# The last phase of a streaming encoder layer: y's scale from a bound, y split and transposed in halves, gates loaded later, two transposes on other PSUM banks

## The chip, the cores and the metric

One core of a Trainium2 chip. The metric is the device time of one execution in microseconds (us). The engines are named as in the profile: PE (TensorE) multiplies, PEld loads its weights, DVE is VectorE, ACT is ScalarE, POOL is GpSimd, SP issues the DMAs.

## The reference

One layer of a chunk-causal encoder for 2048 prompt frames and 8 x 16 sample frames with caches of 512. Each frame is normalised and modulated, projected by `w_in`, and goes through two attention branches (differential and stick-breaking). The last phase of the kernel computes the merge and the output of each frame:

```python
def merge_branches(oa, ob, za, zb, ga, gb, subln_g, lam_init, w_branch_a, w_branch_b, w_out):
    b, s = oa.shape[:2]
    oa = rms_norm(oa, subln_g) * (1.0 - lam_init)
    ya = (oa.reshape(b, s, WIDTH_A) * jax.nn.silu(za)) @ w_branch_a
    yb = (ob.reshape(b, s, WIDTH_B) * jax.nn.silu(zb)) @ w_branch_b
    return (jax.nn.sigmoid(ga) * ya + jax.nn.sigmoid(gb) * yb) @ w_out
...
        xp = xp + gate * merge_branches(oa, ob, za, zb, ga, gb, subln_g[l], lam_init,
                                        w_branch_a[l], w_branch_b[l], w_out[l])
...
    y_prompt = rms_norm(xp, final_g)
```

Below, u is the gated attention output (what the branch weights multiply, 1024 wide), y is the merged sum (what `w_out` multiplies, 1024 wide), and g are the two gates `ga`, `gb`.

## The kernel before

All large products run on PE in 16-bit halves: an operand is scaled by a power of two per row, rounded to 16 bits (the high part), and the rest is rounded too (the low part); a product is three matmuls, high x high, high x low and low x high. `split` makes the two parts: one instruction on the engine given (here ACT) for the high part, one on DVE for the low part. The power of two comes from `scales`, a handful of operations on one column, from the sum of squares of the row, so that nothing overflows.

The kernel goes through eight units of projection and attention, and then, from about 1790 us of the profile on, through the last phase, which is what the diff touches; the tail of the last unit already runs its first tiles (`early_work`). The rows are cut into 17 tiles of 128 frames, in the order `tiles`: 15 prompt tiles, the sample tile, the last prompt tile. Iteration n of the last loop has these pieces of work, written in this order (the document uses the short names):

- b(n), `branches`: four groups of 12 matmuls of 512 columns (L1202), for each column half j both branches br. Each group is scaled and gated on DVE into the gate's own buffer (L1204); after the second branch the two are added on POOL (L1206), which gives a half of y. When both halves are there, `finish` takes their sums of squares on ACT (L274), makes y's scale `sy`, and splits both halves (L287 on ACT, L292 on DVE) into one buffer `y16`.
- T(n+1), `turned`: one DMA transpose of u of the next tile (L1191), 16 blocks of 128 x 128.
- inputs(n+2): loads o_d, z_d (L1158, L1159) and the gates g_d in two halves (L1163); sigmoid of z on ACT into banks of tag mm, products on POOL (L1170) and DVE (L1172, L1176), sigmoid of g on ACT (both L120), sum of squares, scale and split of u. The buffers `hs[0]`, `hs[1]` (o, z) and `hs[2]` (split u) are single.
- o(n-1), `output`: two groups of 24 matmuls of 512 columns (L1335) for the tile before, then the scaling on DVE (L1339), the residual on POOL (L1343), the last norm and the store.
- Ty(n), `turned_y`: one DMA transpose of y's two parts (L1227), 16 blocks, into the single buffer `L["y"]`.

Beside that, `aside(n)` deals out the work of the sample's attention in small steps (`sample`): `keys` turns cached keys on PE (L735), in turn into a PSUM bank of tag t and one of tag s, and copies them out (L736, DVE and ACT); `queries` turns the sample's queries (L721); `weights` turns the attention weights, four blocks in a bank s (L770) and the last block in a bank t (L776). The PSUM has two banks of tag mm, three of tag s, one of tag t and two of tag o. The sample's work lasts for the first 13 of the iterations.

What runs when: `interleave` merges the lists by their shares of cost into one written order. A planner (`schedule_with_timeline_sim=True`) then orders the instructions of each engine and of each queue by its own simulated times, and every engine runs its list strictly in that order. So an instruction that waits holds up all that stand behind it on its engine, and SP's DMAs stand in one such list. The activations that need a table (sigmoid, exp) are tied to each other in their written order (`act`).

Of the kernel before, what the change touches and what calls it, by code (L numbers as in the profile page):

```python
# [25 lines left out]
P = 128  # L26
D = 1024
# [83 lines left out]
def layer_kernel(ctx: ExitStack, tc: tile.TileContext, a: dict):  # L111
# [589 lines left out]
    def sample(U, dec, fixed):  # L701
# [14 lines left out]
            load(out=kc, in_=caches[name][:, i * 8 : i * 8 + 8, h * P : (h + 1) * P])  # L716

        def queries():
            pt = bank("t")
            for j in range(2):  # L720
                T.transpose(pt[:, j * P : (j + 1) * P], box["s"][:, j * P : (j + 1) * P], ident)  # L721
# [44 lines left out]
        def weights(c):  # L766
            w = box["jobs"][c]["segs"][0]["p"]
            pt = bank("s")
            for j in range(4):
                T.transpose(pt[:, j * P : (j + 1) * P], w[:, j * P : (j + 1) * P], ident)  # L770
# [5 lines left out]
            T.transpose(pt[:, 0:P], w[:, 512:640], ident)  # L776
            S.copy(out=wn[:, c, :], in_=pt[:, 0:P])

# [376 lines left out]
    def inputs(t):  # L1155

        o, z = hs[0:2]
        load(out=o, in_=o_d[t])  # L1158
        load(out=z, in_=z_d[t])  # L1159
        gs = []  # L1160
        for j in range(2):
            gs.append(L["g"][(2 * len(begun) + j) % 4].rearrange("p (b n) -> p b n", b=2))
            load(out=gs[j], in_=g_d[t].rearrange("p (b n) -> p b n", b=2)[:, :, j * 512 : (j + 1) * 512])  # L1163
        begun.append(t)
        r = L["orms"][:, 4 * t : 4 * t + 4] if t < NT else rsqrt(osums[:, NT, :], 4, P, tiny, "rA")
        for n in range(2):
            c = slice(n * 512, (n + 1) * 512)
            sg = bank("mm")
            act(out=sg, in_=z[:, c], func=AF.Sigmoid)
            G.tensor_tensor(out=o[:, c], in0=o[:, c], in1=z[:, c], op=ALU.mult)  # L1170
            if n == 1:
                V.tensor_tensor(out=o[:, c], in0=o[:, c], in1=sg, op=ALU.mult)  # L1172
            else:
                for h in range(4):
                    c = slice(h * P, (h + 1) * P)
                    V.scalar_tensor_tensor(out=o[:, c], in0=sg[:, c], scalar=r[:, h : h + 1], in1=o[:, c], op0=ALU.mult, op1=ALU.mult)  # L1176
# [9 lines left out]
        return dict(u16=u16, u=L["u"][len(begun) % 2], iu=iu, g=gs)  # L1186

    def turned(st):

# [3 lines left out]
    def branches(st):  # L1193

        def half(j, br):
# [8 lines left out]
            V.scalar_tensor_tensor(out=g, in0=pb, scalar=st["iu"], in1=g, op0=ALU.mult, op1=ALU.mult)  # L1204
            if br == 1:
                G.tensor_tensor(out=g, in0=st["g"][j][:, 0, :], in1=g, op=ALU.add)  # L1206
                if j == 1:
                    finish()

        def finish():  # L1210
            acc = tiny.tile([P, 2], F32, tag="yacc", name="yacc")
            for j in range(2):
                sum_squares(st["g"][j][:, 1, :], 512, acc[:, j : j + 1])
            sy = scales(add_up(acc, 2), unit, "sy")
            y16 = L["y16"].bitcast(F16).rearrange("p (f n) -> p f n", f=2)
            for j in range(2):
                c = slice(j * 512, (j + 1) * 512)
                split(y16[:, 0, c], y16[:, 1, c], st["g"][j][:, 1, :], sy[:, 0:1], S)
            iy = unit.tile([P, 1], F32, tag="iy", name="iy")
            V.tensor_tensor(out=iy, in0=sy[:, 1:2], in1=L["s"][1][:, 1:2], op=ALU.mult)  # L1220
            st["y16"], st["iy"] = y16, iy

        return [(2.6, lambda j=j, br=br: half(j, br)) for j in range(2) for br in range(2)]

    def turned_y(st):
        st["y"] = yT = L["y"].bitcast(F16).rearrange("p (k n) -> p k n", n=P)
        nc.sync.dma_start_transpose(out=yT, in_=st["y16"].rearrange("p f n -> p (f n)"))  # L1227


    tiles = list(range(NT - 1)) + [NT, NT - 1]  # L1230
# [2 lines left out]
    def branch_weight():  # L1233

        i = branch_weights.pop(0)
        if i == 0:
            L["s"] = [scales(total(add_up(wsums[:, lo : lo + 8], 8)), con, f"s_w{lo}") for lo in (0, 8)]
# [8 lines left out]
    def early_work():  # L1246


        free.extend(units[7]["bufs"])

        def first(t):
            if "orms" not in L:
                L["orms"] = rsqrt(osums[:, 0:NT, :].rearrange("p t h -> p (t h)"), 4 * NT, P, con, "orms")
            states[t] = inputs(t)
            if t == tiles[0]:
                turned(states[t])

        def early(i):

            if i == 0:  # L1260
                L["first"] = [fn for _, fn in branches(states[tiles[0]])] + [lambda: turned_y(states[tiles[0]])]
            L["first"][i]()

        def rest():
            L["g"], L["u"], (L["y"], L["y16"]) = free[0:4], free[4:6], free[6:8]

        return [branch_weight for _ in branch_weights] + [rest] + [lambda t=t: first(t) for t in tiles[0:2]] \
            + [lambda i=i: early(i) for i in range(5)]

    for n in range(first_step, len(steps) + PV_LAG):  # L1270
        if n < len(steps):
# [24 lines left out]
    with ExitStack() as c2:  # L1296
# [25 lines left out]
        def output(t, st):  # L1322
            box = {}

            def half(j):
# [4 lines left out]
                c = slice(j * 512, (j + 1) * 512)  # L1330
                po = bank("o")
                n = 0
                for yi, wi in ((0, 0), (0, 1), (1, 0)):
                    for k in range(KT):
                        T.matmul(po, st["y"][:, yi * 8 + k, :], wo[j * 4 + k // 2][:, wi, k % 2, :], start=(n == 0), stop=(n == 3 * KT - 1))  # L1335
# [39 lines left out]
        for n in range(NT + 2):  # L1375
# [40 lines left out]
```

## Time and profile before

| what | value |
|---|---|
| median of 3 runs | 2296.72 us (2291.05 to 2299.35) |
| the profiled execution | 2301.96 us, span 2300.1 us |
| mean granted TensorE clock | 0.962 |
| busy over the span | PE 91%, DVE 70%, ACT 64%, PEld 48%, POOL 30% |

Rows of the timeline read: start in us, length in us, engine, line, operation, output <- input (buffer numbers left out), partitions x elements, number of instructions, and in brackets the idle time of the engine just before with what ended it. Rows of the waits read: engine and line that waited <- what it waited for: total us, times, longest. A row of windows reads: the window, its length, then the busy time of PE, PEld, DVE, ACT and POOL with counts, the granted clock, the DMA share and GB/s. For an SP row the length is the time of issuing; landing is counted from the issue.

### The profile page before, as it was taken

How to read it: one execution, taken by the hardware profiler on the slowest of the kernel's cores; microseconds unless marked ns; L12 is line 12 of the kernel's file. 1: busy time of each engine (PE TensorE's matmuls, PEld its weight loads, DVE VectorE, ACT ScalarE, POOL GpSimd, SP SyncE). 2: the span in 40 equal slices, each digit the busy share in tenths (PEclk: the TensorE clock that was granted, in tenths of full speed). 3: DMA queues.
4: the chain of work that ended last, by engine and by line, in shares of the span. 5: the costliest groups of instructions: out<-in, count | busy, mean ns of one | idle time of the engine just before them, and what ended most of it. 6: DMA issues, size and time to landing. Idle time of an engine off the chain costs nothing. (4 is left out here: it accounts for less than half of the span.)

```text
span 2300.1 us, 40624 instructions
## 1 busy us (share of the span) xinstructions
PE 2088.9 (91%) x14478; PEld 1111.0 (48%) x14478; DVE 1609.4 (70%) x3523; ACT 1482.1 (64%) x2968; POOL 688.5 (30%) x575
## 2 busy tenths in 40 slices
PE   4997998998999899899989989999986789888997
PEld 2554554554555455455545555555553344444443
DVE  4576866689786677978666798877778655555554
ACT  3876767678776677777667787766776444444431
POOL 1522012345300234530023464113344222232331
PEclk7998999999999999999999999999997899999998
DMA  8659658597775768875566887657687979887662
GB/s 293 209 139 259 169 126 223 143 203 180 195 158 125 164 143 194 183 192 134 116 163 145 198 182 174 150 137 162 149 185 174 300 216 260 209 218 199 185 154 74
DMA packets 764555, 412.98 MB, mean 180 GB/s; under 512 B 525530, under 2 KB 709130, under 8 KB 763840
## 3 DMA queue, kind: packets, MB, share of 16 engines
q1 hardware_dynamic: 763274, 409.91, 72.7%
q8 instruction: 113, 1.85, 0.3%
q14 instruction: 90, 0.74, 0.1%
q10 hardware_dynamic: 1078, 0.48, 0.1%
HBM read 212.58 MB, written 72.91 MB: 124 GB/s over the span
## 5 line engine op out<-in xcount | busy, mean ns | idle before, releaser
L613 POOL TENSOR_TENSOR sc_p<-sc_p,sc_n 128x127 f32<-128x127 f32 (+7 forms) x192 | 307.4, 1605 | 791.6 <-DVE sc_n L607 775.7
L423 PE MATMUL ps_mm<-wb,hs 128*128 128x512 f16 x1632 | 415.8, 386 | 4.2 <-ACT gt L498 4.2
L423 PEld LDWEIGHTS <-hs 128*128 128x128 f16 x2976 | 263.7, 99 | 253.7 <-issue 23.2
L423 PE MATMUL ps_mm<-wa,hs 128*128 128x512 f16 x1344 | 335.8, 381 | 6.0 <-DVE v L292 4.7
L607 DVE TENSOR_TENSOR_SCAN sc_n<-ps_s,sc_n,zero_t 128x512 f32<-128x512 f32 x192 | 245.4, 1278 | 70.5 <-ACT ps_s L120 68.4
L120 ACT ACTIVATE sc_p<-ps_s,usc 128x512 f32<-128x512 f32 (+3 forms) x320 | 202.5, 633 | 104.8 <-PE ps_s L631 62.2
L630 PE MATMUL ps_s<-k,qst 128*128 128x512 f16 (+3 forms) x640 | 226.1, 354 | 45.7 <-DVE sc_n L607 33.5
L562 DVE TENSOR_TENSOR sc_n<-sc_p,sc_n 128x128 f16<-128x128 f32 (+7 forms) x192 | 213.6, 1118 | 43.0 <-ACT sc_n L561 42.6
L1335 PE MATMUL ps_o<-wo,wb 128*128 128x512 f16 x816 | 199.6, 400 | 30.3 <-DMA wb<-wa 25.5
L631 PE MATMUL ps_s<-k,qst 128*128 128x512 f16 (+3 forms) x640 | 226.3, 354 | 0.0
L682 PE MATMUL ps_o<-v,wt 128*128 128x128 f16 x1088 | 192.5, 225 | 26.2 <-DMA wt<-sc_n 26.0
L495 PE MATMUL ps_mm<-wa,hs 128*128 128x512 f16 x816 | 203.3, 379 | 1.2 <-DVE wa L292 1.2
L495 PE MATMUL ps_mm<-wb,hs 128*128 128x512 f16 x816 | 203.2, 379 | 0.0
L495 PEld LDWEIGHTS <-hs 128*128 128x128 f16 x1632 | 140.5, 98 | 123.4 <-issue 1.4
L120 ACT ACTIVATE ps_s<-ps_s,usc 128x512 f32<-128x512 f32 (+3 forms) x320 | 194.0, 606 | 0.0
L561 ACT CAST sc_n<-sc_p 128x128 f16<-128x128 f32 (+7 forms) x192 | 153.6, 804 | 57.3 <-POOL sc_p L613 57.1
L683 PE MATMUL ps_o<-v,wt 128*128 128x64 f16 x1088 | 174.0, 198 | 0.0
L682 PEld LDWEIGHTS <-wt 128*128 128x128 f16 x1088 | 107.3, 101 | 107.0 <-DMA wt<-sc_n 34.9
L1335 PEld LDWEIGHTS <-wb 128*128 128x128 f16 x816 | 81.9, 102 | 135.4 <-DMA wb<-wa 31.1
L457 POOL TENSOR_TENSOR rot<-pr,rope 128x256 f32<-128x256 f32 x68 | 64.2, 944 | 273.6 <-ACT pr L437 225.5
L683 PEld LDWEIGHTS <-wt 128*128 128x128 f16 x1088 | 105.3, 101 | 72.3 <-issue 1.9
L607 DVE TENSOR_TENSOR_SCAN sc_n<-ps_s,zero_t 128x128 f32<-128x128 f32 (+3 forms) x128 | 104.5, 818 | 48.1 <-ACT ps_s L120 46.4
(324 smaller groups left out, 4177.7 us busy)
## 6 DMA issues: line engine op xcount, KB each, us to landing
hs<-hT_d SPq DMA_DIRECT2D x124, 512.0 KB, 4.2
g_d<-gt SPq DMA_DIRECT2D x68, 256.0 KB, 4.1
out_dram<-pr SPq DMA_DIRECT2D x204, 64.0 KB, 1.9
wide<-in_w_ada_dram SPq DMA_DIRECT2D x12, 1024.0 KB, 9.9
wa<-in_w_in_dram SPq DMA_DIRECT2D x36, 256.0 KB, 5.5
z_d<-pr SPq DMA_DIRECT2D x136, 64.0 KB, 2.0
o_d<-o SPq DMA_DIRECT2D x136, 64.0 KB, 2.4
hs<-z_d SPq DMA_DIRECT2D x17, 512.0 KB, 4.1
```

Source lines behind the costliest of these rows:

```text
L120: i = S.activation(**kw)
L423: T.matmul(box["p"], box["h"][:, hi, k, :], U["w"][k][:, wi, :], start=(n == 0), stop=(n == 3 * KT - 1))
L495: T.matmul(box["g"][:, 0:gw], box["h"][:, hi, k, :], U["wg"][k // per][:, k % per, wi, :], start=(j == 0), stop=(j == 3 * KT - 1))
L561: S.copy(out=hi, in_=src)
L562: V.tensor_tensor(out=lo, in0=src, in1=hi, op=ALU.subtract)
L607: V.tensor_tensor_scan(out=dst[:, lo : lo + n][:, ::-1], data0=src[:, 0:n][:, ::-1], data1=zero_t[:, 0:1].to_broadcast([P, n]), initial=fi ...
L613: G.tensor_tensor(out=p[:, 0:m], in0=p[:, 0:m], in1=n[:, 1 : m + 1], op=ALU.mult)
L630: T.matmul(p[:, 0:n], qst[:, c, :], kk[:, c, 0:n], start=True, stop=False)
L631: T.matmul(p[:, 0:n], qst[:, 2 + c, :], kk[:, c, 0:n], start=False, stop=not diag)
L682: T.matmul(po[:, c * P : (c + 1) * P], wt[:, wj, :], vt[:, c, :, :], start=first, stop=False)
L683: T.matmul(po[:, c * P : c * P + 64], wt[:, nb + wj, :], vt[:, c, 0, :], start=False, stop=last)
L1335: T.matmul(po, st["y"][:, yi * 8 + k, :], wo[j * 4 + k // 2][:, wi, k % 2, :], start=(n == 0), stop=(n == 3 * KT - 1))
```

## The change

Five edits, all in the last phase and in the pieces of it that run early.

1. y's scale comes from a bound, not from y: the sum of squares of u (known in `inputs`) times the sum of squares of the branch weights `wf`. `finish` is gone; `sy` and `iy` are made in `inputs`.
2. Each half of y is split as soon as it is added, into the first half of the buffer of its own gates (`home[j]`), and each half is transposed by itself (8 blocks); `y16` is gone.
3. Turned y has two buffers, used in turn. The output matmuls take the blocks of the first column half first, then those of the second, in each group of 24.
4. The loads and sigmoids of the gates are taken out of `inputs` into `gated`, which is written at the end of an iteration, behind both transposes of y; the buffers of g become those that hold y's parts of two tiles before.
5. The sample's queries and last weights use banks of tag s instead of t.

```diff
         def queries():
-            pt = bank("t")
+            pt = bank("s")
...
-            pt = bank("t")
+            pt = bank("s")
             T.transpose(pt[:, 0:P], w[:, 512:640], ident)
...
         load(out=z, in_=z_d[t])
-        gs = []
-        for j in range(2):
-            gs.append(L["g"][(2 * len(begun) + j) % 4].rearrange("p (b n) -> p b n", b=2))
-            load(out=gs[j], in_=g_d[t].rearrange("p (b n) -> p b n", b=2)[:, :, j * 512 : (j + 1) * 512])
...
-        for g in gs:
-            act(out=g, in_=g, func=AF.Sigmoid)
         acc = tiny.tile([P, 1], F32, tag="uacc", name="uacc")
         sum_squares(o, D, acc)
         su = scales(acc, unit, "su")
+        yb = tiny.tile([P, 1], F32, tag="yb", name="yb")
+        V.tensor_tensor(out=yb, in0=acc, in1=L["wf"], op=ALU.mult)
+        sy = scales(yb, tiny, "sy")
+        iy = tiny.tile([P, 1], F32, tag="iy", name="iy")
+        V.tensor_tensor(out=iy, in0=sy[:, 1:2], in1=L["s"][1][:, 1:2], op=ALU.mult)
...
+        m = len(begun) % 2
+        return dict(t=t, u16=u16, u=L["u"][m], iu=iu, sy=sy, iy=iy, home=L["g"][2 * m : 2 * m + 2], yT=L["y"][m])
+
+    def gated(st):
+
+        st["g"] = [b.rearrange("p (b n) -> p b n", b=2) for b in st["home"]]
+        for j in range(2):
+            load(out=st["g"][j], in_=g_d[st["t"]].rearrange("p (b n) -> p b n", b=2)[:, :, j * 512 : (j + 1) * 512])
+        for g in st["g"]:
+            act(out=g, in_=g, func=AF.Sigmoid)
...
                 G.tensor_tensor(out=g, in0=st["g"][j][:, 0, :], in1=g, op=ALU.add)
-                if j == 1:
-                    finish()
-
-        def finish():
-            acc = tiny.tile([P, 2], F32, tag="yacc", name="yacc")
-            for j in range(2):
-                sum_squares(st["g"][j][:, 1, :], 512, acc[:, j : j + 1])
-            sy = scales(add_up(acc, 2), unit, "sy")
...
+                y16 = st["home"][j].bitcast(F16)[:, 0:D]
+                split(y16[:, 0:512], y16[:, 512:D], g, st["sy"][:, 0:1], S)
...
-    def turned_y(st):
-        st["y"] = yT = L["y"].bitcast(F16).rearrange("p (k n) -> p k n", n=P)
-        nc.sync.dma_start_transpose(out=yT, in_=st["y16"].rearrange("p f n -> p (f n)"))
+    def turned_y(st, j):
+        st["y"] = yT = st["yT"].bitcast(F16).rearrange("p (k n) -> p k n", n=P)
+        nc.sync.dma_start_transpose(out=yT[:, j * KT : (j + 1) * KT, :], in_=st["home"][j].bitcast(F16)[:, 0:D])
...
-                for yi, wi in ((0, 0), (0, 1), (1, 0)):
-                    for k in range(KT):
-                        T.matmul(po, st["y"][:, yi * 8 + k, :], wo[j * 4 + k // 2][:, wi, k % 2, :], start=(n == 0), stop=(n == 3 * KT - 1))
+                for half, yi, wi in [(half, yi, wi) for half in range(2) for yi, wi in ((0, 0), (0, 1), (1, 0))]:
+                    for k in range(half * 4, half * 4 + 4):
+                        T.matmul(po, st["y"][:, half * KT + yi * 4 + k % 4, :], wo[j * 4 + k // 2][:, wi, k % 2, :], start=(n == 0), stop=(n == 3 * KT - 1))
...
             if 0 < n <= NT:
-                work.append((0.9, lambda n=n: turned_y(states[tiles[n]])))
+                work.insert(-1, (0.5, lambda n=n: turned_y(states[tiles[n]], 0)))
+                work.append((0.5, lambda n=n: turned_y(states[tiles[n]], 1)))
+            if n + 2 <= NT:
+                work.append((0.1, lambda n=n: gated(states[tiles[n + 2]])))
             interleave(work, aside(n))
```

In the part that runs early, the first two tiles call `gated` straight after `inputs`, and the first tile's two half transposes are pieces of their own.

More of the change, by code (lines that the diff above doesn't have):

```diff
@@ L1185, in inputs @@
         V.tensor_tensor(out=iu, in0=su[:, 1:2], in1=L["s"][0][:, 1:2], op=ALU.mult)
-        return dict(u16=u16, u=L["u"][len(begun) % 2], iu=iu, g=gs)
+        m = len(begun) % 2
[6 more added lines that the diff above has]
+            act(out=g, in_=g, func=AF.Sigmoid)
     def turned(st):
@@ L1236, in branch_weight @@
         if i == 0:
-            L["s"] = [scales(total(add_up(wsums[:, lo : lo + 8], 8)), con, f"s_w{lo}") for lo in (0, 8)]
+            sums = [total(add_up(wsums[:, lo : lo + 8], 8)) for lo in (0, 8)]
+            L["wf"] = con.tile([P, 1], F32, name="wf")
+            V.tensor_copy(out=L["wf"], in_=sums[0])
+            L["s"] = [scales(x, con, f"s_w{lo}") for x, lo in zip(sums, (0, 8))]
             L["sa"] = con.tile([P, 1], F32, name="sa")
@@ L1254, in first @@
             states[t] = inputs(t)
+            gated(states[t])
             if t == tiles[0]:
@@ L1260, in early @@
             if i == 0:
-                L["first"] = [fn for _, fn in branches(states[tiles[0]])] + [lambda: turned_y(states[tiles[0]])]
+                L["first"] = [fn for _, fn in branches(states[tiles[0]])] + [lambda j=j: turned_y(states[tiles[0]], j) for j in range(2)]
             L["first"][i]()
         def rest():
-            L["g"], L["u"], (L["y"], L["y16"]) = free[0:4], free[4:6], free[6:8]
+            L["g"], L["u"], L["y"] = free[0:4], free[4:6], free[6:8]
         return [branch_weight for _ in branch_weights] + [rest] + [lambda t=t: first(t) for t in tiles[0:2]] \
-            + [lambda i=i: early(i) for i in range(5)]
+            + [lambda i=i: early(i) for i in range(6)]
     for n in range(first_step, len(steps) + PV_LAG):
```

7 lines of the change are left out of this document (removed).

## The prediction

> **What bounds the kernel now.** I read the page first for the engine that carries the span, then the waits of that engine in the last phase, then the rows around each of its gaps.
>
> ```profile
> span 2300.1 us, 40624 instructions
> PE 2088.9 (91%) x14478; PEld 1111.0 (48%) x14478; DVE 1609.4 (70%) x3523; ACT 1482.1 (64%) x2968; POOL 688.5 (30%) x575
> 1790.00:2301.00 511.00, 440.27 (x2981) 220.76 (x2979) 280.81 (x747) 204.52 (x380) 140.50 (x105) 0.95 0.76 201
> ```
>
> The third row is the last phase as one window: its length, then busy PE, PEld, DVE, ACT, POOL, then granted clock, DMA share and GB/s. PE is busy 440 of 511 us, DVE 281, ACT 205, POOL 141. So the phase is a PE phase with about 71 us in which PE is not busy, and a change there is worth what it takes from that idle time and from the clock that it costs. Nothing of the diff lies before the last phase but the tail of the last unit, so the other 1790 us stay as they are. The waits of PE in the phase (total, times, longest):
>
> ```profile
> PE ps_o L1335 <- DMA wb<-wa: 25.5, 8, 6.8
> PE ps_t L776 <- DVE dks L736: 10.4, 2, 5.2
> PE ps_t L735 <- DVE dks L736: 6.3, 3, 3.5
> PE ps_s L735 <- DVE dsc L607: 4.9, 2, 2.8
> PE ps_t L721 <- DVE dks L736: 3.2, 3, 1.9
> PE ps_o L1335 <- POOL wo L289: 2.5, 1, 2.5
> ```
>
> The first line is the output matmuls o(n) waiting for turned y; the second and fifth are the sample's last weights and queries waiting for the one bank of tag t, which a copy on DVE has not yet emptied. These three, 39.1 us, are what the diff aims at. Gaps cost more than their length, as these rows of the timeline show (start, length, engine and line, count, idle before in brackets):
>
> ```profile
> 2139.30 10.53 PE L1335 MATMUL ps_o<-wo,wb 128*128 128x512 f16 x48
> 1804.45 8.77 PE L1335 MATMUL ps_o<-wo,wb 128*128 128x512 f16 x28 [6.82 <-DMA wb<-wa]
> 2161.05 5.53 PE L1335 MATMUL ps_o<-wo,wb 128*128 128x512 f16 x17 [3.44 <-DMA wb<-wa]
> 2275.64 7.62 PE L1335 MATMUL ps_o<-wo,wb 128*128 128x512 f16 x23 [3.33 <-DMA wb<-wa]
> 2116.15 0.48 PE L776 MATMUL ps_t<-ident,dsc 128*128 128x128 f32 x1 [5.24 <-DVE dks L736]
> 2116.42 7.03 PE L1335 MATMUL ps_o<-wo,wb 128*128 128x512 f16 x23
> ```
>
> Undisturbed, 48 matmuls take 10.53, or 0.219 each. After the gap of 6.82, 28 take 8.77 where 6.1 would do: 2.6 lost. After 3.44, 17 take 1.8 too long; after 3.33, 23 take 2.6 too long; after 5.24, 23 take 2.0 too long.
>
> **The change, part by part.** Durations are of the profiled execution, 2301.96 us (span 2300.1), which is 5.2 above the median 2296.72; I add the sum to the median.
>
> *y's scale from a bound, and the split in halves.* One tile now, from the sum of y's second half to the transpose:
>
> ```profile
> 2115.58 1.26 POOL L1206 TENSOR_TENSOR wa<-wa 128x512 f32<-128x512 f32 x1 [6.11 <-DVE wa L1204]
> 2116.87 0.63 ACT L274 ACTIVATE junk<-wa 128x512 f16<-128x512 f32 x1 [2.83 <-POOL wa L1206]
> 2117.41 0.19 ACT L274 ACTIVATION_READ_ACCUMULATOR junk<-wa 128x1 f32 x1
> 2118.68 0.70 ACT L287 ACTIVATE wa<-wb,sy 128x512 f16<-128x512 f32 x1
> 2121.65 0.74 DVE L292 SCALAR_TENSOR_TENSOR wa<-wa,sy,wa 128x512 f16<-128x512 f32 x1
> 2124.26 3.22 SPq L1191 DMA_TRANSPOSE wb<-hs  x1
> 2127.54 2.93 SPq L1227 DMA_TRANSPOSE wb<-wa  x1
> 2130.52 0.58 SPq L1158 DMA_DIRECT2D hs<-o_d  x1
> ```
>
> Removed are two squares of a half and their reads on ACT, 2 x (0.63 + 0.19) = 1.64 a tile, 28 us of ACT over 17 tiles, off PE's path by themselves. The addition ends at 2116.84, the last split at 2122.39, 5.55 later; with the scale known beforehand only one ACT half (0.70) and one DVE half (0.74) follow it, 1.5. So the last half is ready 4 us sooner, the first half several us before that. On DVE a column sum goes and one product comes, both on one column: nothing. The scale's small operations move to `inputs`, an iteration or two ahead of their use: nothing.
>
> *Two buffers for turned y, two transposes.* The split ended at 2122.39 and the transpose was issued at 2127.54: u's transpose stood before it. In the last tile it was worse:
>
> ```profile
> 2268.76 0.75 DVE L292 SCALAR_TENSOR_TENSOR wa<-wa,sy,wa 128x512 f16<-128x512 f32 x1
> 2263.11 8.15 PE L1335 MATMUL ps_o<-wo,wb 128*128 128x512 f16 x37
> 2271.29 1.72 SPq L1227 DMA_TRANSPOSE wb<-wa  x1
> ```
>
> The split was done at 2269.5, but the only buffer was read by o of the tile before until 2271.26, and the transpose left at 2271.29. With a second buffer this wait is gone. The seven waits for y other than the first make 25.5 - 6.8 = 18.7, 2.7 each; 4 us from the shorter chain, and the queueing on top, cover them, and o(n) can begin with the 12 matmuls of the first half (2.6 us) before the second has landed. So I take 18.7 for the seven; the lower bound is the last alone, 3.3. The first, 6.82, has another cause close behind it:
>
> ```profile
> 1800.74 1.29 DVE L292 SCALAR_TENSOR_TENSOR wo<-x,s_w,wo 128x1024 f16<-128x1024 f32 x1 [0.92 <-ACT wo L287]
> ```
>
> The output weights of the first column half are complete only at 1802.03, 2.4 before PE started (1804.45), and the other half's are waited for again (the 2.5 of L289 in the list), so what is won before them is largely waited for there. I take 2 of the 6.8. Waits for y: 20.7, between 3.3 and 25.5.
>
> *The clock behind these gaps.* 1.8 and 2.6 of the rows above go with their gaps, and the 2.6 of the first gap by half: 5.7, between 2.6 (last gap alone) and 7.0. The Trainium skill, TensorE: Matmul & The Clock Gate, section What's actually happening, says that the array's clock halves after an idle window of about 3.4 us and is whole again after as long a busy one; by that an estimate is 1.7 lost for each such gap, where the rows show 1.8 to 2.6.
>
> *Half transposes on SP.* 17 more transposes are issued. The nearest rows for smaller ones are those of the attention weights, 2 to 16 blocks; the second fence is y's own 16 blocks:
>
> ```profile
> L568 SPq DMA_TRANSPOSE wt<-sc_n x280: 1176/1779/6712, 197.9 to 1768.7; - x140
> DMA to landing us min/median/max: 2.3/4.3/8.8
> ```
>
> ```profile
> DMA to landing us min/median/max: 4.3/4.8/9.4
> ```
>
> A half has 8 blocks. Between half of a whole (no cost) and the smallest issue seen (1.18 more a tile, 20 on SP in all); it should land in 2.3 to 4.8. SP is not waited for as long as y leaves 4 us sooner: nothing on the path, 0 to 1.2 a tile as bounds. A rule of the Trainium skill speaks against this edit: DMA: Bandwidth & Descriptors, section Rules for kernel authors, wants many small transfers joined into a large one, as small ones pay mostly overhead. By that rule the second rival below comes true, whose price is worked out there from rows. The Trainium skill, Perfetto Trace Analysis, section DMA Optimizations, also allows that smaller pieces start sooner. No row here has a half transpose beside its whole.
>
> *Gates read later.* The loads of g for tile n+2 now wait until both halves of y(n) have left the buffers that they write, so they start 2.3 to 9.4 after the transposes are issued, where today they start with the split. Who needs them:
>
> ```profile
> 2128.21 1.06 ACT L120 ACTIVATE wa<-wa 128x1024 f32<-128x1024 f32 x1 [2.60 <-DMA wa<-g_d]
> 2141.88 0.60 ACT L120 ACTIVATE ps_mm<-hs 128x512 f32<-128x512 f32 x1 [0.84 <-DVE hs L1176]
> ```
>
> Sigmoids and exponentials keep their written order on ACT, so z's sigmoid of the next `inputs` must follow g's. Today 12.6 us lie between them (2129.27 to 2141.88); the delay, less the 4 us that y is earlier, is at most 5.4. Nothing, at worst a few us once or twice.
>
> *Banks s.* Why L776 waited 5.24 at 2110.9: the copy that empties t came at 2115.4. Would an s bank have been free?
>
> ```profile
> 2099.34 0.60 PE L735 MATMUL ps_s<-ident,dk 128*128 128x128 f32 x4
> 2109.66 0.60 PE L735 MATMUL ps_s<-ident,dk 128*128 128x128 f32 x4
> 2110.10 0.60 PE L770 MATMUL ps_s<-ident,dsc 128*128 128x128 f32 x4
> 2112.16 0.58 ACT L736 COPY dks<-ps_s 128x512 f32<-128x512 f32 x1
> ```
>
> No: these three filled the three s banks, and the first was emptied at 2112.74. So of 5.24 some 1.8 stay and 3.4 go, and I take the twin of this wait (10.4 in two) alike: 6.8, between 0 and 10.4; with gaps under 2 us goes the 2.0 of clock behind each: 4.0. Of the 3.2 of the queries I take half, 1.6, between 0 and all. The s banks get 20 more tenants (8 queries, 12 weights) beside keys and scores; waits for s were 4.9 on keys, and I let them grow by that amount: -5, between 0 and -10.
>
> *Planner.* It orders every engine by its own estimate, and the new readiness of y will reorder PE, DVE and ACT. No row prices it; the nearest are PE's small waits for other causes (1.8, 0.7, 0.6 in single cases). I take -2, between +5 and -15.
>
> Sum: 20.7 + 5.7 + 6.8 + 4.0 + 1.6 - 5 - 2 = 31.8. Against the profiled execution 2270.2, against the median 2296.7 - 31.8 = 2264.9; I say 2265. This case by itself runs from 2247 (all waits for y, L776 and L721 gone: 39.1, with 11.0 of clock, no new ones) to 2277, where the first rival begins; all low ends at once would be 3.3 + 2.6 - 10 - 15 = -19, which is 2316 and lies with the slower cases.
>
> **Can the rest keep up?** The loop behind the prefetch runs through SP and hs: o_d is loaded, made into u, u is transposed, and only then is the next o_d issued:
>
> ```profile
> 2100.04 0.57 SPq L1158 DMA_DIRECT2D hs<-o_d  x1
> 2188.07 0.85 SPq L1158 DMA_DIRECT2D hs<-o_d  x1
> ```
>
> Three turns in 88.03, 29.3 each. The removed squares take 1.6 off it, y's transpose, once it leaves before u's, 2.9: 24.8. Of the 31.8 some 22 fall within the tiles that have sample work, about 12: 1.9 each, so PE wants a tile every 27.4. So the loop keeps up, with 2 us to spare.
>
> **Rivals.**
> *The bank stays the trouble.* L776 and L721 wait for s as long as for t, since one late copy (DVE behind L1176) holds both. Then 6.8, 4.0 and 1.6 are missing: 2277. For it: the three filled banks above. Against: the first of them is emptied 3.3 before t is.
> *SP becomes the bound: slower.* If the loads of g stand on SP between u's transpose and o_d, their wait for a landed transpose (4.8) is added to the loop: 24.8 + 4.8 = 29.6, today's pace. Then the gains inside the tiles are lost and only the ends remain, 3.3 + 2.6 + 2 + 1.3 = 9: 2288. If each of the two loads waits for its own half in turn, with 1.2 for the extra issue: 24.8 + 9.6 + 1.2 = 35.6, 6.3 over today on some 12 tiles, +76 - 9: 2364. It decides from a loop of 29.3 on. For it: SP is one queue in order, and today's loads of g already wait on it for the split. Against: in program order o_d's load is written ahead of both transposes and of g, and there are 12.6 us to g's deadline.
> *The split's chain was not the limit.* The planner may keep y's transposes behind u's and o(n) behind the same work, while PE waits for evacuations stuck behind L1176 on DVE instead. Half the gain: 2281.
> *More than expected*: waits of keys for t shrink too, as t has fewer tenants, 6.3 more: 2247 or a little under.
>
> **How the numbers follow.** Forecast 0.50; bank 0.14; chain 0.14; SP at today's pace 0.10; SP slower 0.05; more than expected 0.07. A measurement tells about 0.5% from no change, 11.5 us: faster is under 2285.2, slower over 2308.2. Faster: 0.50 + 0.14 + 0.07 and a good half of the chain's 0.14, 0.79; same: the rest of it and SP at today's pace, 0.15; slower 0.06. The range takes in the forecast's bounds, the bank, the chain and SP at today's pace: 2246 to 2289.
>
> **What would show it.** Right: L1335's wait for turned y falls from 25.5 to about 5, and what stays is the first; the last tile's transposes leave before o of the tile before has ended, with no gap of 3.3; L776 and L721 wait under 2 us at a time; squares of wa and wb are gone from ACT; the window of the last phase has PE busy as long, in some 32 us less. Wrong: o_d's loads 29 us apart or more; z's sigmoid on ACT waiting behind g's load; SP idle with g's load at its head; new waits of PE for tag s of over 10 in all.

## The result, and the profile after

The changed kernel takes 2304.11 us in the median (2294.68 to 2312.42), the kernel before, run on the same chip, 2295.62 (2291.05 to 2299.35): ratio 1.0033, 95% interval 1.0024 to 1.0042. It is slower by some 8 us, which lies inside the half per cent that was called "the same"; the forecast was 2265, with 2246 to 2289 as its range.

The profiled execution at hand of the changed kernel is the fastest of its runs, and that of before lies above all of its own, so their spans don't compare. The lines below are of the changed kernel profiled once more, in a usual execution (2302.91; first experiment below). There the first transpose of u leaves at 1752.21, against 1753.37 before, so the windows match. Its page, and the window of the last phase (length, then busy PE, PEld, DVE, ACT, POOL, granted clock, DMA share, GB/s):

```profile
span 2301.1 us, 40532 instructions
PE 2090.9 (91%) x14478; PEld 1115.4 (48%) x14478; DVE 1604.7 (70%) x3524; ACT 1460.6 (63%) x2900; POOL 689.7 (30%) x575
1790.00:2301.00 511.00, 442.06 (x2977) 224.99 (x2974) 276.99 (x731) 181.92 (x315) 137.82 (x105) 0.93 0.74 200
```

ACT is busy 182 us in place of 205: the squares are gone. PE is busy as long as before (442 against 440), in the same 511 us. The 32 us didn't come. PE's waits in the phase (total, times, longest):

```profile
PE ps_t L735 <- DVE dks L736: 16.6, 5, 6.6
PE ps_s L770 <- ACT dks L736: 7.6, 3, 3.9
PE ps_t L735 <- DMA dk<-in_cache_a_k_dram: 6.2, 2, 4.3
PE ps_s L770 <- POOL dsc L613: 5.7, 1, 5.7
PE ps_mm L1210 <- DVE wb L1212: 5.5, 2, 4.2
PE ps_o L1334 <- DMA x<-in_w_out_dram: 4.9, 1, 4.9
PE ps_s L776 <- ACT dks L736: 3.8, 3, 2.2
```

The waits of the output matmuls (now L1334) for turned y, 25.5 in eight before, are gone altogether. In their place PE waits longer for banks that a copy dks (L736) on DVE or ACT has not emptied, in front of key blocks (L735) and weights (L770, L776): all such waits add up to 31.2, against 19.9 before. The other rows above are new or longer. All gaps of PE over 0.3 us, from 1740 on, add up to 74.1 before and 72.1 here.

Where these copies come late is seen in one tile. These are rows of the timeline, engine by engine: SP's queue, then POOL, ACT, DVE and PE. The split of u that frees o's buffer ends at 2048.1.

```profile
2048.17 0.54 SPq L1192 DMA_DIRECT2D wa<-g_d  x1
2048.80 1.27 SPq L1222 DMA_TRANSPOSE wa<-wb  x1
2050.18 3.61 SPq L1199 DMA_TRANSPOSE wb<-hs  x1
2053.90 0.54 SPq L1192 DMA_DIRECT2D wb<-g_d  x1
2054.49 0.59 SPq L1158 DMA_DIRECT2D hs<-o_d  x1
...
2059.93 2.48 POOL L1166 TENSOR_TENSOR hs<-hs,hs 128x512 f32<-128x512 f32 x2 [6.92 <-DMA hs<-o_d]
2062.38 1.26 POOL L1342 TENSOR_TENSOR x<-m,x 128x512 f32<-128x512 f32 x1
...
2058.53 1.06 ACT L120 ACTIVATE wb<-wb 128x1024 f32<-128x1024 f32 x1 [4.99 <-DMA wb<-g_d]
2063.67 1.06 ACT L274 ACTIVATE junk<-x 128x1024 f16<-128x1024 f32 x1 [3.61 <-POOL x L1342]
2064.73 0.57 ACT L736 COPY dks<-ps_s 128x512 f32<-128x512 f32 x1
...
2064.85 0.15 DVE L255 TENSOR_SCALAR r<-facc 128x1 f32<-128x1 f32 x1 [9.18 <-ACT junk L274]
2065.74 0.68 DVE L736 COPY dks<-ps_t 128x512 f32<-128x512 f32 x1
...
2065.44 1.08 PE L770 MATMUL ps_s<-ident,dsc 128*128 128x128 f32 x4 [3.92 <-ACT dks L736]
```

Read it from the top. On SP, o's load stands behind the transposes and behind g's second load, and leaves 6.4 us after the split. POOL's products wait 6.92 for it, and the residual addition of the output (L1342) stands behind them in POOL's order. ACT waits 3.61 for that addition with a key copy behind it; DVE waits 9.18 for ACT with another key copy behind it. PE waits 3.92 for ACT's copy. Nothing is busy for long; four engines stand in their order behind one load. This is one tile; whether it is the rule for the phase is taken up in experiment 8. Over the phase the products of POOL wait 112.2 us (86.3 before); the first two rows are of the changed kernel, the others of the kernel before:

```profile
POOL hs L1166 <- issue: 69.7, 8, 14.6
POOL hs L1166 <- DMA hs<-o_d: 42.5, 6, 9.9
POOL hs L1170 <- issue: 47.7, 6, 12.5
POOL hs L1170 <- DMA hs<-o_d: 38.6, 5, 12.0
```

### The profile page after: what moved, and what is told of

Same layout as the page of the kernel before. It is cut to its first block, busy times and chain, and to the rows that moved or that the text cites. A ratio compares the mean times of both kernels' runs of the same rounds, so it can differ in the third digit from the quotient of the medians.

```text
span 2292.8 us, 40532 instructions
## 1 busy us (share of the span) xinstructions
PE 2083.5 (91%) x14478; PEld 1111.3 (48%) x14478; DVE 1606.0 (70%) x3524; ACT 1460.7 (64%) x2900; POOL 687.8 (30%) x575
## 5 line engine op out<-in xcount | busy, mean ns | idle before, releaser
L607 DVE TENSOR_TENSOR_SCAN sc_n<-ps_s,sc_n,zero_t 128x512 f32<-128x512 f32 x192 | 245.5, 1278 | 69.3 <-ACT ps_s L120 67.1
L1210 PE MATMUL ps_mm<-wa,wb 128*128 128x512 f16 x510 | 130.0, 393 | 6.4 <-DVE wb L1212 3.7
```

The source lines that it names most:

```text
L607: V.tensor_tensor_scan(out=dst[:, lo : lo + n][:, ::-1], data0=src[:, 0:n][:, ::-1], data1=zero_t[:, 0:1].to_broadcast([P, n]), initial=fi ...
L1210: T.matmul(pb, st["u"][:, ui * 8 + br * 4 + k, :], L["wb"][br * 4 + k // 2 * 2 + j][:, wi, k % 2, :], start=(n == 0), stop=(n == 11))
```

## The experiments

Three theories stood at the start. A: the phase is paced by the chain behind o's load (one buffer for o, one for z), so PE's waits only change their name. B: the bank edit costs what the rest gains. C: reading g later costs, by ACT's stops at g (C1) or by SP's queue (C2). Later ones are stated in the expectations: E is C2 made precise, a lag of o's load behind the split of u, whatever stands between; F and G are about the bound.

Ratios are against the kernel before, run on the same chip beside each. "Lag" is the time from the end of DVE's split of u to the issue of o's next load on SP, averaged over tiles 3 to 13 of the trace. It is 9.1 in the kernel before and 8.0 in the changed one, so it did not grow with the change.

**1. The changed kernel again.** No edit.

> The changed kernel once more, for a profile of a usual execution (the one at hand, 2294.7, is the fastest of its twenty) beside the next three. All theories: 2304 (2298 to 2310), last phase some 8 us longer than in the profile at hand, with no wait of the output matmuls for turned y. The extra time should be spread over PE's waits for copies out of the banks of tags t and s (key copies), not in one place. If instead the output matmuls wait for y again, or one wait of over 10 us stands alone, the gain was not made in the first place.

2302.91 (2302.41 to 2309.62), ratio 1.0029 (1.0017 to 1.0042). No wait for y came back, and the largest single wait is 6.6: more than half of what PE waits for are copies, as shown above. The profiled span is no longer than that of before (2301.1 against 2300.1), so this trace shows where the gain went, not the 8 us of the medians.

**2. The banks.**

```
         def queries():
-            pt = bank("s")
+            pt = bank("t")
...
-            pt = bank("s")
+            pt = bank("t")
             T.transpose(pt[:, 0:P], w[:, 512:640], ident)
```

> The changed kernel with the sample's queries and last weights back on the bank of tag t. Theory B (the bank edit costs what the other edits gain: s banks get 20 more tenants, and PE's waits for s stand at about 20 us in the changed kernel's profile) expects 2292 to 2297, 8 to 12 less than the changed kernel. Theory A (the input loop, which holds one buffer for o and one for z, paces the phase at 32 us a tile, so PE's waits only change their name) expects 2301 to 2307, with waits for t back at 5 to 10 and the waits for s down by as much. Theory C (gates) expects the same as A.

2302.63, ratio 1.0015 (1.0003 to 1.0027). That is 3 us less than 1 by the ratios, where theory B wanted 8 to 12, and the intervals overlap: at most a part of the loss, and not told from nothing.

**3. Gates early.** Edit: `gated` is called beside `inputs` again, and y16 goes elsewhere so that g's buffers are free:

```
-                y16 = st["home"][j].bitcast(F16)[:, 0:D]
+                y16 = st["out"][j].bitcast(F16)[:, 0:D]      # out = [yy, u's own buffer]
...
-            if n + 2 <= NT:
-                work.append((0.1, lambda n=n: gated(states[tiles[n + 2]])))
```

> The changed kernel with g loaded and its sigmoid issued in inputs again, as before; to make this possible y's halves are written to u's own buffer and to one new half buffer, not over g. Theory C (g read later holds SP ahead of o_d and ACT ahead of the copies: ACT waits 97 us for g's loads after, 67 before) expects 2280 to 2290: the other edits then show their gain. Theory A expects 2298 to 2304: g's waits on ACT fall back to about 67 and SP's waits for landed transposes (about 26) go, but o_d's turns stay 31 to 32 us and PE's waits only move. Theory B expects 2304.

2289.22, ratio 0.9964 (0.9949 to 0.9978): 15 us less than the changed kernel (0.0065 of 2299). The key waits `L735 <- DVE dks` fell from 16.6 to 1.1, and lag from 8.0 to 2.2. Whether the gain comes from ACT's stops at g (67.1 here, 100.6 in the changed kernel), from SP's order or from the other place of y16 is not told by this run, since all three changed.

**4. A second buffer for o.** o of tile n+3 is loaded into it ahead; for room, m got one buffer and the gate rows are read into the new buffer.

> The changed kernel with a second buffer for o: o of tile n+3 is loaded while tile n+2 is still made into u; z keeps one buffer (it is free after POOL's products). The copy m gets one buffer in place of two, for room. Theory A expects POOL's wait for o and z (40 us in front of its products) to fall under 15, DVE's and ACT's waits behind POOL to fall with it, and PE's waits for key copies by 15 to 30: 2275 to 2290. Theories B and C expect 2300 to 2306, as neither the banks nor g's loads change. If POOL's wait falls and the time doesn't, the input loop is not what paces PE's waits.

2307.61, ratio 1.0039 (1.0024 to 1.0054). POOL's waits ahead of its products fell to 62.5, from 112.2, and the time didn't fall; PE's waits for copies dks are 27.5. By the expectation's last sentence this speaks against theory A. It is not a clean test, since the room that it needed brought a wait of PE of its own, and DVE waits 9.2 for m's single buffer:

```profile
PE ps_t L1330 <- DMA o<-gate_d: 8.0, 1, 8.0
```

**5. The sigmoids of g later, the loads as they are.** `gated` is cut in two; the sigmoids are written in the next iteration between the pairs of branch matmuls.

> The changed kernel with g's loads where it has them (at the end of the iteration) but g's sigmoids written half an iteration later, in the next iteration between the two pairs of branch matmuls. Loads and buffers stay, so SP holds the same. Theory C1 (the loss is made on ACT: sigmoids and exponentials keep their written order, ACT stops 100 us in all at g's loads and with it the key copies, the splits and the norms' squares behind it) expects ACT's waits for g to fall under 15, PE's waits of key copies (24 us) to fall under 10, and 2278 to 2290. Theory C2 (the loss is made on SP, where g's loads stand with waits for landed transposes) expects 2300 to 2306. Early gates gave 2289; if C1 holds this should be at least as good, as ACT then waits for g less than before the change.

2301.18, ratio 1.0026 (1.0011 to 1.0042). ACT's waits for g fell, from 100.6 to 70.7, about what they were before the change (67.0), and the time didn't. PE's waits for copies dks stayed at 32.5, and lag is 9.1. Run 3 has about the same total of stops at g (67.1) and is 14 us faster, so this total is not what sets the time. C1 is weakened, not ruled out: the planner chose the sigmoids' places, and the stops fell to 70.7 only, not under 15.

**6. Early gates and bank t together.** Edits 2 and 3.

> Early gates as in after_early_gates, and the sample's queries and last weights back on the bank of tag t. In after_early_gates PE waits 14.7 us in two for a bank s held by a score copy on DVE that the bank edit may have made. Theory B' (with the gates out of the way the bank edit costs) expects 2276 to 2284, 5 to 13 less than after_early_gates. The prediction's own term says 7 to 12 more, 2296 to 2301. No effect of the banks: 2286 to 2292.

2283.30, ratio 0.9944 (0.9929 to 0.9959), lag 2.4. Against run 3 (0.9964) the intervals overlap.

**7. Parts of the change alone, in the kernel before.** The scale from the bound, y16 and transpose whole; two buffers for turned y, with y16 in u's own buffer; both.

> The kernel before with one part of the change: y's scale from the bound; y16, one transpose, gates and banks as before. The squares of y's halves are gone from ACT. The prediction's terms: y ready some 3 to 4 us sooner, which takes up to half of the 25.5 us of waits of the output matmuls, 2280 to 2288 with the clock. Theory A (waits only change their name, since the copies are held up elsewhere) expects 2291 to 2297.

> The kernel before with one part of the change: two buffers for turned y, in turn (for room, y's split goes to u's own buffer once its matmuls are done); scale, one transpose, gates and banks as before. The prediction's terms: the last tile's 3.3 with 2.6 of clock, and what the other waits owe to the buffer being read, 2283 to 2291. Theory A: 2292 to 2297 but for the end's 4 to 6 us, so 2289 to 2293. If u's buffer, now held until y is turned, delays the next transpose of u: 2300 or more.

> The kernel before with the scale from the bound and the two buffers for turned y together; whole transpose, gates and banks as before. Singly they gave 2303 and 2299. The prediction's terms for both: 2275 to 2285. Theory A/E (the gain of y's earlier chain is lost in the order that the planner gives to SP and the copies): 2296 to 2306.

2303.45, ratio 1.0034 (1.0019 to 1.0049); 2298.85, 1.0010 (0.9998 to 1.0023); 2307.87, 1.0044 (1.0029 to 1.0059). None gained. The two with y16 in u's buffer have a fault of their own: u's transpose leaves 7.6 and 7.2 us after the split on average (1.1 before), since the buffer is held until y is turned. They are no measure of the second buffer. The run with the bound alone warns against reading the time off the lag: it is 6.9 there, less than in the kernel before, and the time is 8 us more.

**8. SP's order set by hand.** In the changed kernel and in the one before, o's load stands directly ahead of the transpose of u, by its written place and a dependency that only orders; in the changed one g's loads stand behind it too, and g's loads and sigmoids are written half an iteration later, about where 5 had the sigmoids.

```
+    def fetch_o(t):
+        o_in[t] = load(out=hs[0], in_=o_d[t])
+    def behind_o(i, t):
+        if t in o_in:
+            tc.add_manual_dep(i.ins, o_in[t].ins.name, NOSYNC, reason="o first")
...
+        i = nc.sync.dma_start_transpose(out=st["u"], ...)
+        behind_o(i, ahead)
```

> The changed kernel with SP's order alone set by hand: o's load of tile n+3 stands directly ahead of the transpose of u(n+2), and g's loads of tile n+2 behind it. In the changed kernel o's load is issued 7.9 us on average after the split of u that frees its buffer (tiles 3 to 13; g's load, which waits for y's landed transposes, and u's transpose stand ahead of it), with early gates 2.0. Theory E (the lag between the split of u and o's load is what costs: POOL's products wait for o and everything on POOL, ACT and DVE behind them comes late) expects a lag under 2, POOL's waits for o 112 us to about 85, PE's waits of key copies down by half, and 2285 to 2294. Theory C1 (ACT stopped at g's loads): g comes no sooner than now, so 2300 to 2306. Neither: within 3 us of 2303.

> The kernel before with SP's order alone set: o's load of tile n+2 directly ahead of the transpose of u(n+1). Its lag after the split is 2 to 18 us today, 8.5 on average. Theory E expects 2284 to 2291 here too, without anything of the change. If it holds only in the changed kernel, 2294 to 2299: then the lag costs only where y's chain is already out of the way.

2282.59, ratio 0.9935 (0.9923 to 0.9947), and 2282.34, ratio 0.9935 (0.9923 to 0.9947). Lags: 1.3 and 0.7. Both times lie a little under the ranges that theory E gave. So o's place on SP is worth 15 us in the kernel before, where nothing else was edited, and 21 in the changed kernel, whose loss is gone with it. The kernel before had most of this loss already. Tile 2, outside the average, has a lag of 18.8 in the changed kernel and 3.3 with o first (21.1 and 15.2 in the kernel before), so a part is won there. SP's rows at the same tile (split's end 2034.2), and the waits of POOL's products (64.4 in place of 112.2), in the changed kernel with o first:

```profile
2035.61 1.23 SPq L1234 DMA_TRANSPOSE wa<-wb  x1
2036.93 0.53 SPq L1158 DMA_DIRECT2D hs<-o_d  x1
2037.56 4.63 SPq L1210 DMA_TRANSPOSE wb<-hs  x1
2042.29 0.55 SPq L1202 DMA_DIRECT2D wa<-g_d  x1
```

```profile
POOL hs L1176 <- DMA hs<-o_d: 32.4, 7, 7.4
POOL hs L1176 <- issue: 32.0, 7, 6.1
```

o's load comes 2.7 after the split. ACT's waits for g are 82.6 in all, 18 less than in the changed kernel but more than in run 3 (67.1), which is slower by 7 us; so they don't set the time here either.

What keeps o's load back is mostly not g. Of the lag of 8.0 in the changed kernel 4.1 is u's own transpose, 1.7 the sample's transfers, 1.3 g's loads with the idle time ahead of them, 0.5 y's transposes; of the 9.1 before, 4.4, 1.5, 0.1 and 2.7.

The path from o's load to PE is shown in part only. PE's waits for copies dks fall with the time, from 31.2 to 11.5, and in the kernel before from 19.9 to 6.7. These are the two rows left in the changed kernel with o first:

```profile
PE ps_s L776 <- ACT dks L736: 6.4, 2, 3.2
PE ps_s L770 <- ACT dks L736: 5.1, 1, 5.1
```

But POOL's waits were as low in run 4 (62.5), with 2307.61. And the chain of the tile above did not get shorter over the phase: ACT's wait for the residual addition and DVE's wait for ACT, first in the changed kernel, then with o first, both rose.

```profile
ACT junk L274 <- POOL x L1342: 34.8, 9, 9.9
DVE r L255 <- ACT junk L274: 58.7, 13, 10.0
ACT junk L274 <- POOL x L1354: 58.1, 9, 9.9
DVE r L255 <- ACT junk L274: 72.6, 13, 12.4
```

So that the order costs is shown; that it costs by way of this chain is not.

With the order set the two kernels take the same time, though one still waits for y and the other doesn't. In the kernel before with o first the longest line of PE's waits is still

```profile
PE ps_o L1346 <- DMA wb<-wa: 21.9, 9, 6.6
```

**9. The bound once more, with o first.** All with o first. In the kernel before: the scale from the bound; the bound's seven small operations on DVE added but not used. In the changed kernel: these operations held back behind DVE's part of u's split.

> The kernel before with the scale from the bound and SP's order set as in before_o_first. before_bound alone gave 2303, 0.34% over before, although the waits for y fell from 25.5 to 18.9. Theory E expects that the order takes the loss away and the bound's own gain shows: 2278 to 2288, below before_o_first by 3 to 8. If the loss of the bound is its own (the scale's small operations ahead of u's split on DVE), 2290 to 2300, above before_o_first by 5 or more.

> before_o_first with the bound's seven small operations on DVE added in inputs and their result not used; the squares of y's halves and the scale from them stay. Theory F (the small operations ahead of u's split cost: they lie in the chain o, u, split, o's load) expects the 12 us of before_bound_o_first over before_o_first, so 2291 to 2296. Theory G (they cost nothing; without the squares the planner gives ACT and DVE another order, and that costs) expects 2280 to 2285.

> after_o_first with the same seven operations held back behind DVE's part of u's split. Theory F expects 2268 to 2276, 7 to 14 less than after_o_first (2282.6). Theory G expects 2280 to 2285.

2294.63, ratio 0.9984 (0.9975 to 0.9992); 2280.98, 0.9931 (0.9912 to 0.9949); 2284.11, 0.9947 (0.9932 to 0.9962). The small operations cost nothing, and holding them back gains nothing: theory F falls. The bound alone still costs 11 us (0.9984 against 0.9935). A trace of it points to the single y16 buffer, for which the earlier split now waits on ACT, with the copies behind it:

```profile
ACT wa L287 <- DMA wb<-wa: 17.2, 4, 8.1
```

In the profile of before, and in that of before_o_first, that wait is 2.4. This is a reading of one row; no run took it away, and the cause stays open.

**10. Bank t, and early gates, with o first.**

> after_o_first with the sample's queries and last weights back on the bank of tag t. With early gates this gave 2283.3 against 2289.2, 5 us less (by the ratios), with the changed kernel alone 3 less. If the bank edit costs by itself: 2275 to 2280. If those two were the planner's accidents: within 3 us of 2282.6, or over it.

> after_early_gates_t (2283.3) with o's load set directly ahead of the transpose of u. There the lag after the split is 0 to 5.5 us already, 2.4 on average, so theory E expects 1 to 6 us less: 2277 to 2283. If the gain of the early chain was held back only by the order, as the prediction's sum would have it: 2265 to 2272.

2284.94, ratio 0.9953 (0.9936 to 0.9970): with the order set, bank t is no better. The three pairs that differ in the banks alone give -0.14%, -0.20% and +0.18%, each with overlapping intervals: the bank edit can't be told from nothing. The second has early gates, bank t and the order set: 2278.26, ratio 0.9916 (0.9900 to 0.9931). Against the first, which has late gates and y16 over g but the same banks and order, that is 8 us less, with intervals apart. With all obstacles out of the way the early y is worth 0.0019 of 2297, 4 us, against before_o_first, with intervals that overlap. Setting the order changed the lag little in this version (2.4 to 2.3), yet the time is 6 us under run 6, with intervals that just overlap: another sign that the average lag does not measure what costs.

**11. The residual addition off POOL.** In the version with all obstacles away, and in before_o_first:

```
-                G.tensor_tensor(out=x[:, c], in0=m, in1=x[:, c], op=ALU.add)
+                V.tensor_tensor(out=x[:, c], in0=m, in1=x[:, c], op=ALU.add)
```

> early_gates_t_o_first (2278) with the residual addition of the output on DVE in place of POOL, where it stands behind o's products, which wait 88 us for o. Theory A (copies of banks come late because the norm's chain, POOL, ACT, DVE, holds ACT and DVE in order) expects ACT's wait of 56 us for that addition to fall under 15, PE's waits of key, query and weight copies (16 us) by half, and 2262 to 2272, although DVE gets 34 additions of some 0.7 us more. If DVE's own work sets the copies, the 24 us more on it cost: 2280 to 2290. If neither: 2275 to 2281.

> before_o_first (2282) with the same addition on DVE. Its waits for turned y (21.9 us in nine) stay. Theory A expects less here than with the early y, 2274 to 2282, as the waits for y take the place of the waits for copies. If DVE's own work sets the copies: 2284 to 2292.

2269.78, ratio 0.9872 (0.9854 to 0.9889), and 2276.29, ratio 0.9899 (0.9882 to 0.9917): 10 and 8 us less by the ratios, although DVE does more (290 us in the window 1790 to 2301 in place of 276). ACT's wait for that addition, before and after the edit:

```profile
ACT junk L274 <- POOL x L1355: 56.1, 10, 9.9
```

```profile
ACT junk L274 <- DVE x L1355: 24.4, 7, 9.5
```

It fell by half, not under 15, and PE's gaps over 0.3 us from 54.1 to 50.0. POOL's products now wait 184 in place of 87.7, and it costs nothing that can be seen. The time came out as theory A had it, but its path only in one of the two kernels: PE's waits for copies of keys, queries and weights, which were to halve, stay at 14.0 in the first, and go from 9.9 to 3.7 in the second. That the addition's place on POOL costs is shown; through what, is open. The first of these is the fastest version found, 28 us under the kernel before; the early y's share in it is 6 us (0.9872 against 0.9899, intervals overlapping).

## Why the prediction was wrong, point by point

*Waits for y.* Right as a mechanism: 25.5 to none, where 5 were to stay. The first wait, where the output weights were to be waited for instead, indeed became 4.9 for their load (L1334 in PE's list). The last tile's half transposes leave before o(15) has ended, with no gap ahead of the last output matmuls (SP's row, then PE's):

```profile
2272.49 1.24 SPq L1222 DMA_TRANSPOSE wa<-wb  x1
2268.51 8.15 PE L1334 MATMUL ps_o<-wo,wb 128*128 128x512 f16 x37
2276.50 0.38 PE L1334 MATMUL ps_o<-wo,wa 128*128 128x512 f16 x1
```

Wrong was the step that took these waits at their length: 20.7 in the sum, with 5.7 of clock. PE's waits for copies rose from 19.9 to 31.2 instead, and with SP's order set alike a kernel that waits 21.9 for y takes the same time as one that doesn't (run 8); with the gates early as well, early y was worth 4 to 6 us, with intervals that overlap (runs 10 and 11). This is the failed step that weighs most. The third rival ("the split's chain was not the limit", copies stuck on DVE instead) described it, and was given 0.14 and half the gain. That it is L1176 on DVE that holds the copies, as it said, is not shown.

*Clock.* 5.7 were to be saved; the granted clock of the window went from 0.95 to 0.93, as the new gaps are as long. Behind the gap of 3.92 above,

```profile
2052.13 2.75 PE L1210 MATMUL ps_mm<-wa,wb 128*128 128x512 f16 x12
2068.45 1.06 PE L1210 MATMUL ps_mm<-wb,wb 128*128 128x512 f16 x2
2070.73 2.75 PE L1210 MATMUL ps_mm<-wb,wb 128*128 128x512 f16 x12
```

two matmuls take 1.06 where twelve take 2.75, and full pace is back only 5.3 us after the gap's end at 2065.44; the granted clock of these 5.3 us is 0.51. The size per gap was right; the gaps only moved.

*Half transposes on SP.* Right, with room. From 1790 to 2190 SP spends 46.5 us on 24 half transposes, where 13 whole ones took 51.6, and a half lands in 3.2 in the median, a whole in 4.8:

```profile
DMA to landing us min/median/max: 3.1/3.2/7.5
```

The rule of the Trainium skill (DMA: Bandwidth & Descriptors, section Rules for kernel authors) to join many small transfers says that under 64 KB one pays mostly overhead. A half is 256 KB by its shape (128 x 1024 elements of two bytes), so the prediction took the rule beyond that size. No cost of the split shows in this trace.

*Gates read later: "nothing".* This step failed too. With the gates early the changed kernel is 15 us faster (run 3). That is not the price of the move alone, as the kernel before, whose gates are early, has a loss of 15 on SP as well: run 3 has an order that neither had, with o's load ahead of u's transpose in most tiles. With that order set by hand and the banks alike the late gates cost 8 us (run 10). So the move was not free, and the rest of the 15 is the planner's order. The prediction looked at a deadline on ACT alone. The second rival looked at SP, with 0.10 and 0.05, and set itself aside since o's load is written ahead of g's. The order that it feared is there: in seven of the eleven tiles a load of g stands between u's transpose and o's load. Its price isn't: 1.3 us a tile, where a landed transpose of 4.8 was to be waited for. Written order did not decide on SP; the planner's did, and it was not known.

*"Can the rest keep up?"* The loop was said to take 29.3 a turn, from three turns that happened to be short. From the row below to the last one shown in the prediction (2188.07) there are eleven turns, 32.0 each; in the changed kernel, from 1829.98 to 2188.20, eleven of 32.6.

```profile
1836.15 0.57 SPq L1158 DMA_DIRECT2D hs<-o_d  x1
```

y's transpose did leave the place ahead of o's load (2.7 to 0.5), but g's loads took 1.1 more, and the lag fell by 1.1 only, where 2.9 a turn were counted. So the loop, at 32 a turn, did not have the 2 us to spare. That its turn sets the time is not shown: with o first, at 15 and 21 us less, the same eleven turns are 31.0 each in the kernel before and 32.4 in the changed one.

*Banks.* L776's waits fell from 10.4 to 3.8 and L721's from 3.2 to none, as said. But the waits of L770 for a copy out of a bank s, 7.6, are new, and three pairs of runs show no gain from the edit where 7.4 were forecast (6.8, 4.0 and 1.6, less 5).

*Planner: -2.* The order that it gave to SP is worth as much as any edit tried: 15 us before and 21 after (run 8), so some 6 of it belong to the change. The new order could not be read from the trace of before, and deserved a range that reached a slower case, not 0.05.

*The last rival's sum.* "6.3 more" than the forecast of 2264.9 is 2258.6, not 2247.

Three of the signs that the prediction listed as wrong were seen: o's loads over 29 us apart, waits for tag s of over 10 (17.1 by the three rows of L770 and L776 above), and SP idle ahead of g's loads, 0.5 us a tile. What stands on SP ahead of o's load was the thing to read first, and in the trace of before it could be read.

## What to carry to other kernels

A wait of the bounding engine is worth its length only if whatever it would reach next is ready; list the wait behind it (here: banks that wait for copies) before adding the waits up. Look in each queue for what stands ahead of the load that refills a single buffer, and if a planner makes the order, fix the one pair that matters by hand: one load set ahead of one transpose gave 15 us in the kernel before, without any of the change. Then look whether the waits that should have shrunk did; a chain read in one tile can be a chain of that tile. A loop's period is read from the first and last of all its turns, not from a stretch of three.

## What the runs showed that was not expected

Seven more operations of 0.15 us a tile on DVE, in the middle of the chain from o to u, cost nothing that can be measured (0.9931 against 0.9935); what hides them is not shown. And the same program reached the first transpose of u at 1743.85 in one execution and at 1752.21 in another, 8.4 us apart, and took 548.9 from there to the end of the span in both; a single profile can't tell a difference of that size, and the two phases are to be compared from a common point.
